# Head writes issued from GpSimd and three attentions run as one sequence, in a fused streaming-encoder layer

## The chip, the cores and the metric

The kernel runs on one core of a Trainium2 chip. The metric is device time in microseconds (us) of one launch. The engines are named as the profile names them: PE (TensorE matmul), PEld (its weight loads), DVE (VectorE), ACT (ScalarE), POOL (GpSimd) and SP (SyncE, which here only issues DMAs).

## The reference

One layer with shared weights is computed for a prompt of 2048 rows and for a sample group of 8 x 16 rows that has caches. All is float32, with a model width of 1024.

```python
h = rms_norm(x, g1) * (1 + sc1) + sh1
cols = h @ w_in                    # columns of four mixers A, B, C, D, 4 heads of 64 each
oa = gated_delta_rule(cols_A)      # conv, chunked triangular solve, recurrent state
ob = stick_breaking(q, k, v)       # sigmoid(z) * running product of sigmoid(-z), strictly causal
oc = softmax(q k / 8 + f_q - f_k) v            # causal, forget bias f
od = softmax(q k / 8 + bias[rel]) v            # own chunk of 64 and 8 before it
mixed = concat(oa, *[rms_norm(o_head, merge_g) for o in (ob, oc, od)])
x = x + ga1 * (mixed @ w_o)
h = rms_norm(x, g2) * (1 + sc2) + sh2
a, b = split(causal_conv3(h @ w_up))           # the samples continue from state_ffn_conv
x = x + ga2 * ((silu(a) * b) @ w_down)
```

The outputs are x of both groups and the new caches and states.

## The kernel before

**Parts and streams.** The prompt is cut into four parts of 512 rows; the 128 sample rows go with the first part of the projection and with the last part of the feed-forward. Two generators emit the program. The *dense* stream is the projection of all parts (`proj_stage`, then `feed_stage`): for each part the product with `w_o`, the second norm, 44 column blocks of `w_up` with the convolution (`up`), and the products with `w_down` (`down`). Each float32 product is three matmuls of split values (hi*hi, hi*lo, lo*hi); in the first feed-forward part the split weights are written to DRAM (`keptw_up`, `keptw_down`, `keptw_o`) and in later parts they are loaded from there in pieces of 512 KB. The *mixers* stream (`mixers`) is for each part the delta rule and the attentions B, C, D of the prompt (`attn_prompt`), and in parts 1 to 3 the attention of the samples (`attn_samples`).

**Order of the work.** `weave` takes a step of the mixers, adds its pace (table `PACE`) to a debt and then takes dense steps until the debt is paid. A scheduler in the build then sets the order of the instructions on each engine; mixers have high priority. While part 3's mixers run, `Order.step` ties each dense step to the mixers step 12 before it (`LAG`). A part's feed-forward needs all of that part's `mixed` rows.

**An attention of a part.** Each call of `attn_prompt` opens a tile pool of its own and runs *units*: a head times two blocks of 128 queries (for B also times a segment of 512 keys). `front` of a unit computes scores (PE, tile `z`), and for B (`Stick.segment`) two sigmoids `sn` and `w` on ACT (L733, L734), a running product `pr` on DVE (L741) that starts from the earlier segment's `pr`, and a product on POOL (L743); for C and D (`Soft`) a sum with the bias tile `add` and a maximum on DVE (L773), then exponentials on ACT. `back` of the unit before runs beside it: transposes of the weights (`ptr`), split copies `wh` and `wl`, matmuls with V (`oT`), and for a head's last unit `head_norm`. At a head's end `start_k` loads the next head's `qT`, `kT` and `add`; `start_v` loads `vhl`. At the end of an attention the last `back` runs alone, the pool is closed, and the next attention opens its own.

**`head_norm`** (L863 to L875) loads the gain `hg` (one buffer), squares the head's rows into `nsq` (one buffer, POOL, L869), sums, takes a reciprocal root in 12 small POOL instructions (L214 to L217), scales (L873, L874), and writes `nsq` to `mixed` in DRAM with a DMA of 128 KB issued by SP (L875). SP issues everything in one order, so what stands behind an instruction that waits, waits as well.

**Tiles of the attentions.** `sn` has 2 buffers, `pr` 3, the bias of C one tile of up to 2048 columns, that of D two tiles of 640, `kT` and `vhl` have (segments + 1) buffers, but 4 for C in part 3; `w` has 6 (B), 12 and 11 (C in parts 2 and 3) and 8 (D).

**Others that the change touches.** `samples_steps` loads 512 cached keys at a time into `ck` (512 KB, one buffer) and transposes them in two PSUM tiles, one for each half of the columns. `up` in part 3 loads 16 rows of `state_ffn_conv` into `stn` (two buffers) and transposes them on PE (`ptr<-ident,stn`).

Of the kernel before, what the change touches and what calls it, by code (L numbers as in the profile page):

```python
# [15 lines left out]
P = 128  # L16
# [702 lines left out]
class Stick:  # L719
# [5 lines left out]
    def segment(self, c0, c1):  # L725
# [137 lines left out]
def head_norm(K, A, gi, h, oh, nt, dst):  # L863
# [11 lines left out]
    nc.sync.dma_start(out=dst, in_=sq)  # L875


def attn_prompt(K, g, part):


    nc = K.nc
    gi = "BCD".index(g)
    lo = (lambda i: max(0, i - 4)) if g == "D" else (lambda i: 0)
    mask = {"B": K.m_strict, "C": K.m_incl, "D": None}[g]
    j0, s0, s1 = 2 * part, lo(4 * part) // 4, part + 1
    A = Ctx()
    A.ev, A.pb, A.sb, A.vb = Eng(nc, 0.5), 3, 2, 2 + int(part > 1)
# [11 lines left out]
    def head(h):  # L899
# [4 lines left out]
        H.oh = A.sp.tile([P, 4, 64], F32, name="oh", bufs=2)  # L904
        if g == "C":
            fb = A.sp.tile([P, s1 * 512], F32, name="add", bufs=1)
            nc.sync.dma_start(out=fb.rearrange("p (t c) -> p t c", c=P),
                              in_=K.nF[0:16 * s1].rearrange("(t h) p -> h t p", h=4)[h:h + 1].to_broadcast([P, 4 * s1, P]))
            H.add = lambda a, b, c1: fb[:, a:b]
# [50 lines left out]
    def back(u):  # L960
# [6 lines left out]
        if u.last:  # L967
            u.st.V.finish(None if g == "B" else [w.rl for w in u.st.wts], H.oh, 4 * part)
            if jj == j0 + 1:
                yield  # L970
                r, c = 4 * part * P, (1 + gi) * 256 + H.h * 64
                head_norm(K, A, gi, H.h, H.oh, 4, K.mixed[r:r + 512, c:c + 64].rearrange("(t p) d -> p t d", p=P))

    units = []
    for h in range(4):
        hs = Ctx()
        hs.h = h
        for jj in (j0, j0 + 1):
            st = Ctx()
            for s in range(jj // 2, -1, -1) if g == "B" else [None]:  # L980
# [10 lines left out]
                u.end = u.last and jj == j0 + 1  # L991
                units.append(u)

    def start_k(u):
        H = u.hs.H = head(u.hs.h)
        for s in order:
            H.kT[s] = A.sp.tile([P, 512], F32R, name="kT", bufs=A.ring)
            nc.sync.dma_start(out=f(H.kT[s]).unsqueeze(1), in_=rows(K.kT[g][s], H.h))
        yield

    def start_v(u):
        H = u.hs.H
        for s in order:
            H.v[s] = A.sp.tile([P, 4, 2, 64], F32R, name="vhl", bufs=A.ring)
            nc.sync.dma_start(out=f(H.v[s]).rearrange("p t c d -> p (t c d)"), in_=K.vhl[g][H.h, s])
        yield

    with K.tc.tile_pool(name=f"a{g}{part}", bufs=2, side="right", reuse_waits="tile") as A.sp:
        yield from start_k(units[0])
        for n, u in enumerate(units):  # L1010
            u.H = u.hs.H
            parts = [(front(u), u.nf)]
            if n:
                b = units[n - 1]
                parts.append((back(b), len(b.groups) + b.last))
            yield from merge(*parts)
            if u.start:
                yield from start_v(u)
            if u.end and n + 1 < len(units):
                yield from start_k(units[n + 1])  # L1020
        yield from back(units[-1])
# [457 lines left out]
def attn_samples(K, g, beside):  # L1479

    A = Ctx()
    A.ev, A.wb, A.pb, A.sb = Eng(K.nc, 0.5), 2, 2, 1
# [6 lines left out]
def samples_steps(K, A, g):  # L1489
# [10 lines left out]
    for n, src in (("k", K.qs[g]), ("v", K.ks[g])):  # L1500
        t = sp.tile([P, 4 if n == "k" else 2, 256], F32, name="c" + n, bufs=1 if n == "k" else 2)[:, 0]
# [28 lines left out]
    def load(b, s):  # L1530

        t = sp.tile([P, 4, 256], F32, name="ck", bufs=1)
        nc.sync.dma_start(out=t, in_=ck[0, b, s * 512:(s + 1) * 512].rearrange("(t p) h d -> p t (h d)", p=P))
        return t
# [7 lines left out]
    def keys(L, b, s):  # L1542

        L.kT[s] = []
        for u in range(2):
            k = load(b + u, s)
            kT = sp.tile([P, 2, 512], F32, name="ckT", bufs=2)
            L.kT[s].append(kT)
            for x in range(2):
                pt = psum()  # L1550
                for j in range(4):
                    K.pe.transpose(pt[:, j * P:(j + 1) * P], k[:, j, x * P:x * P + P], K.ident)
                A.ev.copy(kT[:, x], pt)
                yield
# [216 lines left out]
def feed_block(K, B, sa, sp, nxt, pool, copies):  # L1771
# [112 lines left out]

    def up(fi):
# [6 lines left out]
        if smp:  # L1892
            us = u[:, 2 + Tp:2 + Tp + NB * 18].rearrange("p (b s) -> p b s", s=18)
            parts.append((lambda i: us[:, :, i:i + 16], s16(yv[:, Tp:T])))
            stn = sp.tile([16, P], F32, name="stn", bufs=2)
            nc.sync.dma_start(out=stn, in_=I["state_ffn_conv"][0, :, :, fi * P:(fi + 1) * P].rearrange("b r c -> (b r) c"))
# [132 lines left out]
def mixers(K, G, p):  # L2029
# [20 lines left out]
    if p == 0:  # L2050
        yield from B
# [4 lines left out]
        yield from rest()  # L2056
    elif p == 1:
        yield from beside(B, 79, 1)
        yield from rest()
        yield from samples()  # L2060
    else:
        yield from samples()
        yield from B
        yield from rest()
# [97 lines left out]
```

## Time and profile before

| what | value |
|---|---|
| median of 3 runs | 3899.07 us (3897.04 to 3899.76) |
| the profiled execution | 3892.44 us, its span 3890.7 us |
| PE busy | 3628.3 us, 93% of the span |
| DVE, ACT, POOL busy | 2437.3, 1537.0, 1406.7 us |
| mean granted TensorE clock | 0.967 |

Busy time is the union of an engine's instructions; what PE lacks to the span is idle time, and only that can be gained without removing matmuls. A granted clock of 0.5 means that matmuls then run at half rate, so a stall costs its own length and some more. A row of waits tells which instruction waited and what came last before it could start. "DMA kT<-kTD" is a transfer into tile `kT`; its row in the timeline is the issue, not the landing. The stretches in the table of windows are: projection with parts 0 and 1 of the mixers (0 to 1150), samples B and C beside the first feed-forward part (to 1870), part 2's attentions (to 2430), samples D, delta rule and attention B of part 3 (to 2960), C (to 3200), D and the step to the last feed-forward part (to 3330), and that part (to the end).

### The profile page before, as it was taken

Reading aid. Unit: us, or ns where it says so; the run is one execution under the profiler, and the core shown is the slowest. Engines: PE = TensorE matmul, PEld = TensorE weight load, DVE = VectorE, ACT = ScalarE, POOL = GpSimd, SP = SyncE. Lnnn points to the kernel's source line nnn. Section 1 sums busy time; section 2 is a strip of 40 time slices with the busy share of each in tenths; the row PEclk is TensorE's granted clock in tenths of the full one; section 3 lists DMA queues with packets and bytes.
Section 4 is the critical chain, followed back from the end, with each engine's and each line's share of the span. In section 5 each row is a group of like instructions: output and inputs, shape, how many; then the busy total and the mean of one; then the engine's idle time right before and its main releaser. Section 6 shows DMA issues by size and latency. Waiting matters only on the chain.

```text
span 3890.7 us, 66224 instructions
## 1 busy us (share of the span) xinstructions
PE 3628.3 (93%) x22763; PEld 3147.3 (81%) x22763; DVE 2437.3 (63%) x5592; ACT 1537.0 (40%) x3352; POOL 1406.7 (36%) x3487
## 2 busy tenths in 40 slices
PE   6998899989988999999999999989999987899999
PEld 4887889989986667767877888668887876899999
DVE  5668556465676876877595656755875665344344
ACT  3455223343454533543463533413553443232221
POOL 4456244363333444434571112323652122122121
PEclk7999999999998999999999999999999998899999
DMA  7887868877668798987536555665445545444442
GB/s 225 290 279 245 300 199 299 295 256 246 218 227 255 254 307 274 306 293 270 200 120 213 171 201 169 226 209 178 158 148 182 177 123 206 141 149 137 153 143 93
DMA packets 529077, 830.36 MB, mean 213 GB/s; under 512 B 112651, under 2 KB 351260, under 8 KB 528477
## 3 DMA queue, kind: packets, MB, share of 16 engines
q1 hardware_dynamic: 527269, 825.16, 64.2%
q8 instruction: 181, 2.97, 0.3%
q0 software_dynamic: 1472, 0.97, 0.1%
q14 instruction: 155, 1.26, 0.1%
HBM read 611.81 MB, written 224.16 MB: 215 GB/s over the span
## 4 chain that ended last, share of the span: by engine, by line
PE 62%; DMA 11%; DVE 9%; POOL 4%; issue 3%; ACT 2%; SPq 1%; POOLq 0%; DVEq 0%; ACTq 0%
PE d L89 44%; PE z L89 5%; PE oT L89 5%; PE ptr L92 4%; PE ptr L89 2%; PE d L92 1%; DVE pr L741 1%; DMA w<-win 1%; DMA add<-nF 1%; DVE gy L1184 1%; DVE cv L1913 1%; DMA wraw<-in_ada_w_dram 1%; DMA raw<-in_x_prompt_dram 1%; PE z L92 1%; DVE acc L1823 1%
## 5 line engine op out<-in xcount | busy, mean ns | idle before, releaser
L89 PE MATMUL d<-hh,wu 128*128 128x512 f32 (+1 forms) x3520 | 1013.9, 364 | 2.8 <-DMA wu<-keptw_up 1.6
L89 PEld LDWEIGHTS d<-hh,wu 128*128 128x128 f32 x3520 | 635.2, 190 | 94.6 <-issue 8.6
L89 PE MATMUL d<-w,hh 128*128 128x256 f32 (+2 forms) x3536 | 679.3, 288 | 30.3 <-DMA w<-win 9.7
L89 PE MATMUL d<-hl,wu 128*128 128x512 f32 (+1 forms) x1760 | 638.8, 363 | 0.8 <-DVE hl L1863 0.7
L89 PEld LDWEIGHTS d<-w,hh 128*128 128x128 f32 x3536 | 557.6, 191 | 48.6 <-DVE w L459 11.8
L89 PE MATMUL d<-gh,wd 128*128 128x512 f32 (+1 forms) x1760 | 529.8, 369 | 10.3 <-DVE acc L1823 8.1
L89 PE MATMUL d<-w,hl 128*128 128x256 f32 (+2 forms) x1768 | 502.3, 286 | 0.2 <-DVE hl L408 0.2
L1913 DVE SCALAR_TENSOR_TENSOR cv<-u,fcw,cv 128x512 f32<-128x512 f32 (+1 forms) x440 | 300.1, 705 | 174.2 <-ACT cv L1911 170.9
L1823 DVE SCALAR_TENSOR_TENSOR acc<-d,mod,acc 128x512 f32<-128x512 f32 (+2 forms) x432 | 280.8, 656 | 188.4 <-PE d L89 187.1
L89 PEld LDWEIGHTS d<-hl,wu 128*128 128x128 f32 x1760 | 334.0, 190 | 43.9 <-DVE hl L1863 3.0
L89 PEld LDWEIGHTS d<-gh,wd 128*128 128x128 f32 x1760 | 319.1, 189 | 60.3 <-DVE acc L1823 13.6
L89 PEld LDWEIGHTS d<-w,hl 128*128 128x128 f32 x1768 | 336.3, 191 | 4.8 <-issue 3.3
L89 PE MATMUL d<-gl,wd 128*128 128x512 f32 (+1 forms) x880 | 319.4, 363 | 0.0
L89 PE MATMUL z<-kT,qT 128*128 128x512 f32 (+3 forms) x864 | 255.8, 385 | 34.7 <-DMA kT<-kTD 13.8
L840 ACT CAST wh<-ptr 128x512 fp32r<-128x512 f32 (+1 forms) x372 | 197.4, 552 | 226.8 <-PE ptr L92 133.6
L841 DVE TENSOR_TENSOR wl<-ptr,wh 128x512 fp32r<-128x512 f32 (+1 forms) x372 | 232.3, 639 | 79.5 <-ACT wh L840 69.1
L1900 ACT COPY u<-d 128x512 f32<-128x512 f32 (+1 forms) x220 | 109.9, 500 | 396.5 <-PE d L89 391.0
L92 PE MATMUL ptr<-ident,w 128*128 128x128 f32 x1448 | 225.1, 277 | 18.9 <-POOL w L743 8.2
L741 DVE TENSOR_TENSOR_SCAN pr<-sn,pr,zeros 128x512 f32<-128x512 f32 (+3 forms) x172 | 217.8, 1275 | 24.3 <-ACT sn L733 18.8
L1915 POOL COPY hal<-u 128x2 f32<-128x2 f32 x176 | 44.5, 254 | 519.7 <-ACT u L1900 516.2
L743 POOL TENSOR_TENSOR w<-w,pr 128x512 f32<-128x512 f32 (+3 forms) x168 | 190.8, 1138 | 112.1 <-DVE pr L741 60.2
L790 ACT ACTIVATE w<-w,nm 128x512 f32<-128x512 f32 (+3 forms) x284 | 174.1, 615 | 120.5 <-DVE nm L783 98.1
(610 smaller groups left out, 7116.5 us busy)
## 6 DMA issues: line engine op xcount, KB each, us to landing
wu<-keptw_up SPq DMA_DIRECT2D x264, 512.0 KB
w<-win SPq DMA_DIRECT2D x132, 512.0 KB
wd<-keptw_down SPq DMA_DIRECT2D x132, 512.0 KB
keptw_up<-wu SPq DMA_DIRECT2D x88, 512.0 KB
wu<-keptw_o SPq DMA_DIRECT2D x48, 512.0 KB
win<-w SPq DMA_DIRECT2D x44, 512.0 KB
raw<-in_w_up_dram SPq DMA_DIRECT2D x88, 256.0 KB
keptw_down<-wd SPq DMA_DIRECT2D x44, 512.0 KB
```

The costliest lines, as they stand in the source:

```text
L89: return self.note(self.nc.tensor.matmul(out, lhsT, rhs, **k))
L92: return self.note(self.nc.tensor.transpose(*a, **k))
L741: nc.vector.tensor_tensor_scan(out=pr[:, 0:m][:, ::-1], data0=sn[:, :m][:, ::-1], data1=K.zeros[:r, :m], initial=carry, op0=ALU.mult, op1= ...
L743: nc.gpsimd.tensor_tensor(w[:, :m], w[:, :m], pr[:, 1:m + 1], op=ALU.mult)
L790: self.K.nc.scalar.activation(w, w, AF.Exp, bias=self.nm, accum_out=self.l[:, s:s + 1])
L840: nc.scalar.copy(wh[:, c0:c1], pt[:, c0:c1])
L841: nc.vector.tensor_tensor(wl[:, c0:c1], pt[:, c0:c1], f(wh[:, c0:c1]), op=ALU.subtract)
L1184: nc.vector.scalar_tensor_tensor(yc, tap(c, i), self.cw[:, c, i:i + 1], yc, op0=ALU.mult, op1=ALU.add)
L1823: nc.vector.scalar_tensor_tensor(acc[k][:, c0:m], ps[:, :m - c0], gate[:, k, 0:1], acc[k][:, c0:m], op0=ALU.mult, op1=ALU.add)
L1900: nc.scalar.copy(u[:, 2 + c0:2 + m], ps[:, :m - c0])
L1913: nc.vector.scalar_tensor_tensor(o, tap(i), cw[:, i:i + 1], o, op0=ALU.mult, op1=ALU.add)
L1915: nc.gpsimd.tensor_copy(K.hal[:, fi], tail)
```

## The change

1. **Head writes.** `head_norm` issues the write to `mixed` from POOL. The gain `hg` (now 2 buffers) is loaded with the head's `qT`.
2. **One sequence.** In parts 2 and 3 B, C and D are one call of `attn_prompt(K, "BCD", p)`: one pool, one list of units, so that `start_k` of C's first head is emitted at the end of B's last unit, and B's last `back` runs beside C's first `front`; likewise C and D. `kT` and `vhl` have 4 buffers, `w` 10. `sn`, `pr`, C's bias and D's bias share one ring `aux` of 5 tiles of 640 columns. Parts 0 and 1 keep three calls and their buffers.
3. **C's bias** is loaded in pieces of 512 columns (one per segment) instead of in one DMA.
4. **Cached keys** of the samples come in two tiles of 256 keys (`ck`, two buffers); each is transposed into one PSUM tile.
5. **`stn`** is loaded three blocks ahead (four buffers).

The core of the diff:

```diff
@@ Stick.segment
-        sn = A.sp.tile([P, 512], F32, name="sn", bufs=A.sb)[:r]
+        sn = A.aux("sn", 512)[:r]
         w = A.w(m)[:r]
-        pr = A.sp.tile([P, 520], F32, name="pr", bufs=A.pb)[:r]
+        pr = A.aux("pr", 520)[:r]
@@ head_norm
-    mg = A.sp.tile([P, 64], F32, name="hg", bufs=1)
-    nc.sync.dma_start(out=mg, in_=K.I["merge_g"][0, gi, h:h + 1].to_broadcast([P, 64]))
...
-    nc.sync.dma_start(out=dst, in_=sq)
+    nc.gpsimd.dma_start(out=dst, in_=sq)
@@ attn_prompt
+def attn_prompt(K, gs, part):
+    A = Ctx()
+    A.ev, A.vb = Eng(K.nc, 0.5), 2 + int(part > 1)
+    A.psum = lambda: K.mps("z")
+    A.w = lambda m: A.sp.tile([P, 512], F32, name="w", bufs=A.wb)
+    if len(gs) > 1:
+        A.ring, A.wb = 4, 10
+        A.aux = lambda name, n: A.sp.tile([P, 640], F32, tag="aux", name=name, bufs=5)[:, :n]
+    else:
...
+    with K.tc.tile_pool(name=f"a{gs}{part}", bufs=2, side="right", reuse_waits="tile") as A.sp:
+        units = [u for g in gs for u in attn_units(K, A, g, part)]
+        a, b = units[0], units[-1]
+        yield from lab(K.nc, f"{a.g}{part}", a.start_k(a))
+        for n, u in enumerate(units):
+            yield from lab(K.nc, f"{u.g}{part}", attn_unit(units, n))
+        yield from lab(K.nc, f"{b.g}{part}", b.back(b))
+
+def attn_unit(units, n):
+    u = units[n]
+    u.H = u.hs.H
+    parts = [(u.front(u), u.nf)]
+    if n:
+        b = units[n - 1]
+        parts.append((b.back(b), len(b.groups) + b.last))
+    yield from merge(*parts)
+    if u.start:
+        yield from u.start_v(u)
+    if u.end and n + 1 < len(units):
+        yield from units[n + 1].start_k(units[n + 1])
@@ head, in attn_units
+        H.mg = A.sp.tile([P, 64], F32, name="hg", bufs=2)
+        nc.sync.dma_start(out=H.mg, in_=K.I["merge_g"][0, gi, h:h + 1].to_broadcast([P, 64]))
         if g == "C":
-            fb = A.sp.tile([P, s1 * 512], F32, name="add", bufs=1)
...
+            fb = [A.aux("add", 512) for _ in range(s1)]
+            for s in range(s1):
+                nc.sync.dma_start(out=fb[s].rearrange("p (t c) -> p t c", c=P),
...
-            bias = A.sp.tile([P, 640], F32, name="add", bufs=2)
+            bias = A.aux("bias", 640)
@@ samples_steps: load
-        t = sp.tile([P, 4, 256], F32, name="ck", bufs=1)
...
+        ts = [sp.tile([P, 2, 256], F32, name="ck", bufs=2) for _ in range(2)]
+        for n, t in enumerate(ts):
+            c = s * 512 + n * 256
...
@@ feed_block
+    for _ in range(3):
+        state_load()
...
-            stn = sp.tile([16, P], F32, name="stn", bufs=2)
...
+            stn = state.pop(0)
+            state_load()
@@ mixers
     else:
         yield from samples()
-        yield from B
-        yield from rest()
+        yield from attn_prompt(K, "BCD", p)
```

How this moves instructions is shown at three places, all in part 3. First the queue of SP where attention D follows C (`qTD`, `kTD`, `skew` are D's; `wu` and `wd` are weights of the dense stream). Before:

```order
L1801 DMA wu<-keptw_up 128x1024 x6
L875 DMA mixed<-nsq 128x4x64
L903 DMA qT<-qTD 128x1024
L912 DMA add<-skew 128x640
L998 DMA kT<-kTD 128x512 x2
L1005 DMA vhl<-vhlD 128x512 x2
```

and now:

```order
L1015 DMA kT<-kTC 128x512
L937 DMA qT<-qTD 128x1024
L1830 DMA wu<-keptw_up 128x1024
L940 DMA hg<-in_merge_g_dram 128x64
L949 DMA bias<-skew 128x640
L1830 DMA wu<-keptw_up 128x1024 x2
L1978 DMA wd<-keptw_down 128x1024 x2
L1022 DMA vhl<-vhlC 128x512 x2
L1978 DMA wd<-keptw_down 128x1024 x2
L1015 DMA kT<-kTD 128x512
```

Before, D's first loads stood behind the write of C's last head; now that write is not in this queue, and D's loads stand among the last loads of C.

Second, PE at the end of part 3's attentions (`oT<-...,os` is the last attention matmul, `raw` are the rows of `mixed` and of x for the last feed-forward part, `mh` and `ml` its first product). Before:

```order
L89 MATMUL oT<-wl,vhl 128x256
L89 MATMUL oT<-j_676,os 128x64 x2
L92 MATMUL ptr<-ident,stn 128x16 x4
L92 MATMUL d<-ident,raw 128x128 x80
L89 MATMUL d<-mh,wu 128x320
```

and now (the rows left out are `d<-gh,wd` and `d<-gl,wd`, with those shown 39 matmuls in all):

```order
L89 MATMUL oT<-j_676,os 128x64 x2
L89 MATMUL d<-gh,wd 128x512 x3
...
L89 MATMUL d<-gh,wd 128x512
L92 MATMUL d<-ident,acc 128x128 x16
L89 MATMUL d<-gh,wd 128x512
...
L89 MATMUL d<-gh,wd 128x512
L92 MATMUL d<-ident,acc 128x128 x16
L92 MATMUL d<-ident,raw 128x128 x80
L89 MATMUL d<-mh,wu 128x320
```

What is left of the third feed-forward part now stands behind the last attention matmul, and the transposes of `stn` are gone from this place.

Third, the queue of SP at the same place (`keptw_o` are the weights of the first product). Before:

```order
L1735 DMA out_dram<-raw 128x512 x4
L1801 DMA wu<-keptw_o 128x1024 x8
L1896 DMA stn<-in_state_ffn_conv_dram 16x128 x2
L867 DMA hg<-in_merge_g_dram 128x64
L875 DMA mixed<-nsq 128x4x64
L1937 DMA wd<-keptw_down 128x1024 x6
L1896 DMA stn<-in_state_ffn_conv_dram 16x128 x2
L875 DMA mixed<-nsq 128x4x64
L1896 DMA stn<-in_state_ffn_conv_dram 16x128
L1690 DMA raw<-mixed 128x512 x8
```

and now:

```order
L1764 DMA out_dram<-raw 128x512 x4
L1719 DMA raw<-mixed 128x512 x7
L1764 DMA out_dram<-raw 128x512 x3
L1719 DMA raw<-mixed 128x512 x3
L1764 DMA out_dram<-raw 128x512
L1719 DMA raw<-in_x_prompt_dram 128x512 x4
L1719 DMA raw<-in_x_sample_dram 128x512
L1719 DMA raw<-in_x_prompt_dram 128x512
L1830 DMA wu<-keptw_o 128x1024
L1719 DMA raw<-in_x_prompt_dram 128x512
L1830 DMA wu<-keptw_o 128x1024
L1719 DMA raw<-in_x_prompt_dram 128x512 x2
```

The weights of the first product, which stood ahead of the last two head writes, now stand behind the rows of `mixed`.

More of the change, by code (lines that the diff above doesn't have):

```diff
@@ L971, in back, with start_k, start_v @@
                 r, c = 4 * part * P, (1 + gi) * 256 + H.h * 64
-                head_norm(K, A, gi, H.h, H.oh, 4, K.mixed[r:r + 512, c:c + 64].rearrange("(t p) d -> p t d", p=P))
+                head_norm(K, A, H.mg, H.oh, 4, K.mixed[r:r + 512, c:c + 64].rearrange("(t p) d -> p t d", p=P))
+    def start_k(u):
+        H = u.hs.H = head(u.hs.h)
+        for s in order:
+            H.kT[s] = A.sp.tile([P, 512], F32R, name="kT", bufs=A.ring)
+            nc.sync.dma_start(out=f(H.kT[s]).unsqueeze(1), in_=rows(K.kT[g][s], H.h))
+        yield
+    def start_v(u):
+        H = u.hs.H
+        for s in order:
+            H.v[s] = A.sp.tile([P, 4, 2, 64], F32R, name="vhl", bufs=A.ring)
+            nc.sync.dma_start(out=f(H.v[s]).rearrange("p t c d -> p (t c d)"), in_=K.vhl[g][H.h, s])
+        yield
     units = []
@@ L991, in attn_prompt @@
                 u.end = u.last and jj == j0 + 1
+                u.g, u.front, u.back, u.start_k, u.start_v = g, front, back, start_k, start_v
                 units.append(u)
[L994 to L1021, printed above, removed]
+    return units
 def gate_tiles(K, cp):
@@ L1481, in attn_samples @@
     A = Ctx()
-    A.ev, A.wb, A.pb, A.sb = Eng(K.nc, 0.5), 2, 2, 1
+    A.ev, A.wb = Eng(K.nc, 0.5), 2
+    A.aux = lambda name, n: A.sp.tile([P, n], F32, name=name, bufs={"sn": 1, "pr": 2}[name])
     A.psum = lambda: K.mps("ptr")
@@ L1500, in samples_steps @@
     for n, src in (("k", K.qs[g]), ("v", K.ks[g])):
-        t = sp.tile([P, 4 if n == "k" else 2, 256], F32, name="c" + n, bufs=1 if n == "k" else 2)[:, 0]
+        t = sp.tile([P, 2, 256], F32, name="c" + n, bufs=2)[:, 0]
         nc.sync.dma_start(out=t, in_=src)
@@ L1545, in keys @@
         for u in range(2):
[L1546 removed]
             kT = sp.tile([P, 2, 512], F32, name="ckT", bufs=2)
             L.kT[s].append(kT)
[L1549 removed]
+            for n, k in enumerate(load(b + u, s)):
                 pt = psum()
[L1551 to L1553 removed]
+                for x in range(2):
+                    for j in range(2):
+                        c = (2 * x + j) * P
+                        K.pe.transpose(pt[:, c:c + P], k[:, j, x * P:x * P + P], K.ident)
+                A.ev.copy(kT[:, :, n * 256:n * 256 + 256], pt.rearrange("p (x n) -> p x n", x=2))
                 yield
@@ L1883, in carry, with state_load @@
         late.clear()
+    state, ahead_of = [], [c for j in range(NF) for c in (j, NF + j)] if smp else []
+    def state_load():
+        if ahead_of:
+            fi = ahead_of.pop(0)
+            state.append(sp.tile([16, P], F32, name="stn", bufs=4))
+            nc.sync.dma_start(out=state[-1], in_=I["state_ffn_conv"][0, :, :, fi * P:(fi + 1) * P].rearrange("b r c -> (b r) c"))
+    for _ in range(3):
+        state_load()
     def up(fi):
@@ L2055, in mixers @@
         yield from rule
-        yield from rest()
+        yield from chain(*[attn_prompt(K, g, p) for g in "CD"])
     elif p == 1:
-        yield from beside(B, 79, 1)
-        yield from rest()
+        yield from beside(attn_prompt(K, "B", p), 79, 1)
+        yield from chain(*[attn_prompt(K, g, p) for g in "CD"])
         yield from samples()
```

33 lines of the change are left out of this document (13 added, 20 removed).

## The prediction

> **What bounds the kernel now.** I read the page first, then the table of windows by stage, then the waits of PE in the stages that lack most, then the timeline there.
>
> ```profile
> span 3890.7 us, 66224 instructions
> PE 3628.3 (93%) x22763; PEld 3147.3 (81%) x22763; DVE 2437.3 (63%) x5592; ACT 1537.0 (40%) x3352; POOL 1406.7 (36%) x3487
> ```
> ```profile
> core 0: us, PE busy (x) PEld busy (x) DVE busy (x) ACT busy (x) POOL busy (x), PEclk, DMA share, GB/s
> 0.00:1150.00 1150.00, 1046.57 (x8101) 979.10 (x8101) 711.67 (x1805) 472.63 (x1056) 512.29 (x1462) 0.96 0.77 258
> 1150.00:1870.00 720.00, 670.46 (x3603) 503.11 (x3604) 520.17 (x1077) 314.17 (x625) 299.51 (x569) 0.96 0.83 276
> 1870.00:2430.00 560.00, 544.31 (x2896) 457.41 (x2894) 372.75 (x809) 245.06 (x534) 193.13 (x467) 0.98 0.54 178
> 2960.00:3200.00 240.00, 226.55 (x1223) 191.25 (x1222) 145.61 (x372) 107.06 (x242) 34.13 (x114) 0.97 0.56 170
> 3200.00:3330.00 130.00, 90.55 (x539) 77.70 (x539) 73.27 (x258) 47.94 (x133) 28.17 (x115) 0.83 0.56 195
> 3330.00:3891.00 561.00, 550.60 (x3685) 535.35 (x3683) 242.95 (x591) 132.32 (x310) 115.76 (x296) 0.99 0.41 132
> ```
>
> PE is the bound: it lacks 262 us of the span (3890.7 - 3628.3), and the change removes no matmul. So its gain is idle time of PE, and the half clock that follows it. Most of the 262 lies where the change does little: 103 us before 1150. In the stages whose attentions it rebuilds, part 2 lacks only 16 us of 560; attention C of part 3 lacks 13 of 240; attention D with the step to the last feed-forward part lacks 39 of 130, at a granted clock of 0.83. The last part lacks 10 of 561, so earlier `stn` loads can gain nothing once it runs. The waits of PE from 2960 to 3330 name the stalls:
>
> ```profile
> PE ptr L92 <- DMA stn<-in_state_ffn_conv_dram: 18.3, 2, 9.6
> PE z L89 <- DMA kT<-kTD: 13.8, 1, 13.8
> PE z L89 <- DVE mx L773: 5.8, 5, 2.3
> PE z L89 <- DMA kT<-kTC: 5.3, 1, 5.3
> ```
>
> The first of these stands for something else. Transposes of `stn` were queued on PE where the attentions end, but without them PE would have waited there all the same, as the timeline of the last heads shows:
>
> ```profile
> 3283.64 3.96 SPq L1801 DMA_DIRECT2D wu<-keptw_o  x8
> 3287.12 0.66 PE L89 MATMUL oT<-j,os 128*128 128x64 f32 x4 [0.52 <-DVE os L71]
> 3287.82 0.47 DVE L860 TENSOR_SCALAR oh<-oT,rl 128x64 f32<-128x64 f32 x2 [0.75 <-PE oT L89]
> 3291.83 0.39 SPq L875 DMA_DIRECT2D mixed<-nsq  x1
> 3298.88 0.61 POOL L869 TENSOR_TENSOR nsq<-oh 128x256 f32<-128x256 f32 x1 [8.78 <-DMA mixed<-nsq]
> ...
> 3304.45 0.72 POOL L874 TENSOR_TENSOR nsq<-nsq,hg 128x256 f32<-128x256 f32 x1 [0.54 <-DMA wd<-keptw_down]
> 3305.20 0.39 SPq L875 DMA_DIRECT2D mixed<-nsq  x1
> 3307.26 4.22 SPq L1690 DMA_DIRECT2D raw<-mixed  x8
> 3310.01 2.03 PE L92 MATMUL d<-ident,raw 128*128 128x128 f32 x8 [2.98 <-DMA raw<-mixed]
> 3327.49 0.41 PE L89 MATMUL d<-mh,wu 128*128 128x320 f32 x1
> ```
>
> The write of the third head, issued behind 4 MB of weights, took 7.05 us to free `nsq` (3291.83 to 3298.88); only then could the last head be normed, written and read back. PE, with nothing else queued, had its last attention matmul at 3287.12 and its first product of the next part at 3327.49, 40.4 us later.
>
> **The change part by part.** *The end of part 3 (one sequence, order on PE and SP).* Now 39 matmuls of 512 columns and 32 transposes stand behind the last attention matmul. Their rates:
>
> ```profile
> 2702.24 19.13 PE d L89 x84
> ```
> ```profile
> 3278.23 0.82 PE L92 MATMUL d<-ident,acc 128*128 128x128 f32 x6
> ```
>
> 39 x 19.13/84 = 8.9 us and 32 x 0.82/6 = 4.4 us, together 13.3 us of work that was elsewhere and now fills the hole. The chain from the last attention matmul stays: to the end of L860 1.2 us (3288.29 - 3287.12), from L869 to the end of L874 6.3 us (3305.17 - 3298.88), the issue and landing of the write, and from the first read of `mixed` to the first product 20.2 us (3327.49 - 3307.26). SP's last write took 2.06 us from issue to that read. For a DMA issued by POOL the nearest rows are these small loads, and the slowest one:
>
> ```profile
> L293 POOL DMA_DIRECT2D abia<-in_ada_b_dram x16: 520/587/611, 72.8 to 494.0; - x16
> ...
> DMA to landing us min/median/max: 2.7/5.1/6.3
> ```
> ```profile
> smask<-in_smask_dram POOLq DMA_DIRECT2D x1, 90.0 KB, 11.0
> ```
>
> The issue costs 0.6 us. For the landing I take 8 us, between 5.1 (9 KB) and 11.0 (90 KB), nearer to the latter in size (bounds 2.7 and 11.0). The Trainium skill ("DMA: Bandwidth & Descriptors", section "Anatomy of one DMA — SWDGE (gpsimd) path") fits such a DMA as 2.0 us plus bytes / 436e3, which as an estimate for 128 KB is 2.3 us. By it the sum would gain 5.7 us more, but the trace's 5.1 us for only 9 KB does not agree. The weights `keptw_o` now come behind the rows: two pieces behind 16 pieces of 256 KB are 5.2 MB, at the 308 GB/s of this row 17 us, so hidden by the 20.2; for all eight pieces, 8.4 MB, 27 us.
>
> ```profile
> 3292.00:3320.00 28.00, 9.65 (x45) 8.10 (x45) 7.24 (x15) 5.23 (x10) 3.70 (x14) 0.51 0.87 308
> ```
>
> I add 2 us (0 to 7). So 1.2 + 6.3 + 0.6 + 8 + 20.2 + 2 = 38.3 us, and the gain is 40.4 + 13.3 - 38.3 = 15.4 us (7 to 23).
>
> *D's start.* D's loads stood on SP behind the write of C's last head:
>
> ```profile
> 3208.84 0.37 SPq L875 DMA_DIRECT2D mixed<-nsq  x1
> 3210.34 0.86 SPq L998 DMA_DIRECT2D kT<-kTD  x2
> 3215.05 1.83 PE L89 MATMUL z<-kT,qT 128*128 128x512 f32 x4 [13.76 <-DMA kT<-kTD]
> ```
> ```profile
> 3203.00:3221.00 18.00, 5.95 (x16) 4.88 (x17) 3.28 (x10) 0.00 (x0) 4.44 (x22) 0.53 0.62 217
> ```
>
> They now stand among C's last loads, with weights of the dense stream between them. The wait of 13.8 goes, and of the 5.95 us of matmuls at clock 0.53 about 2.5 are lost to the clock: 16.3 us. What is late next is the back of C's last unit, which has dense matmuls beside it; if these are used up earlier, some 4 us return (12 to 16).
>
> *C's start.* 5.3 us and about 2 of clock, 7 us (4 to 8). *C's heads.* The bias came as one tile of 1 MB that had to be free as a whole; now the first piece has the ring's fifth tile, the others follow segment by segment. Of the 5.8 us behind L773 and some 2 of clock I take half, 4 us (0 to 8).
>
> *Part 2.* Its starts are covered by dense work already; these waits from 1870 to 2500 bear on it, and I take 2 us (0 to 5):
>
> ```profile
> PE d L89 <- DMA wu<-keptw_up: 1.6, 1, 1.6
> ...
> PE z L89 <- DMA kT<-kTC: 1.1, 1, 1.1
> ```
>
> *Cached keys.* From 1150 to 1870 PE waited for them and their copies 10.2 us:
>
> ```profile
> PE ptr L92 <- DMA ck<-in_cache_sb_k_dram: 7.1, 2, 3.6
> ...
> PE ptr L92 <- DVE ckT L71: 3.1, 2, 2.3
> ```
>
> Two half tiles let one land while the other is transposed; DMA is 0.83 busy there, so I take half, 5 us (0 to 11).
>
> *What it costs.* POOL issues 48 writes of 0.6 us, 28 us on an engine that is 36% busy, and SP loses as many; none lies ahead of a waiting POOL instruction, since the write follows L874 in its own queue. I take 1 us (0 to 5). The shared ring costs B: tiles are taken in the order sn, pr, sn, pr, so `sn` of a segment takes the tile of the `pr` three segments back, which the scan of the segment just before still reads as its start. So ACT can't run ahead of DVE, which it did:
>
> ```profile
> 2812.46 0.60 ACT L733 ACTIVATE sn<-z 128x512 f32<-128x512 f32 x1 [3.48 <-PE z L89]
> 2813.69 1.36 DVE L741 TENSOR_TENSOR_SCAN pr<-sn,pr,zeros 128x512 f32<-128x512 f32 x1
> 2816.07 0.65 ACT L733 ACTIVATE sn<-z 128x512 f32<-128x512 f32 x1
> ```
>
> The 112 segments of parts 2 and 3 (48 and 64) then need 0.60 + 1.36 us in turn, some 2 us, and in these rows they are 3.6 us apart (2812.46 to 2816.07). PE's dense matmuls cover the rest; I take 4 us (0 to 67, the rival below).
>
> The sum: 15.4 + 16.3 + 7 + 4 + 2 + 5 - 1 - 4 = 45 us. The profiled execution, 3892.44 us with its span of 3890.7, would be 3847; it lies 6.6 below the median of the runs, 3899.07, and from that the time is 3854 us.
>
> **The rivals.** *The shared ring stops B (slower).* Every `sn` waits for the scan before it, behind the dense stream's ACT and DVE work, PE meets the late weights in its fixed order, and no dense matmul stands in between: 112 x 0.60 = 67 us. With the other terms (49) that is 3899 - 49 + 67 = 3917 us. It decides from 57 us of such waits on, when the kernel is slower by 0.2%. For it: DVE is the busiest engine after PE, and the rows above show ACT ahead by 2.6 us (this `sn` began at 2812.46; with the ring it would wait for the scan that ends at 2815.05). Against: segments 3.6 us apart leave 1.6 us of slack in each. Chance 0.07.
>
> *The stalls come back inside C and D.* Loads, bias pieces and weights now share SP's queue closely, and a piece that waits for its tile holds the weights behind it; the gains other than D's start cancel against new waits of 1 to 3 us at heads: 45 - 27 = 18 us, 3881 us. For it: the order shows a weight between almost any two loads of an attention. Against: the windows show DMA 0.56 busy. Chance 0.20.
>
> *Software writes land late.* `nsq` has one buffer, so the next L869 holds POOL until the write has landed, and the last chain holds PE. At twice the slowest row, 22 us, the end of part 3 loses 14: 3868 us. The Trainium skill (same page, section "SWDGE vs HWDGE vs iDMA") says that POOL's descriptors are written to rings in SBUF, from which a busy DVE can lock it out, and so speaks against this edit; no row here shows 128 KB written that way. Chance 0.09.
>
> *New waits eat all of it,* within 0.2%: 0.07. That the change doesn't do what it says is out: the order shows it.
>
> **How the numbers follow.** About 0.2%, 7.8 us, is what a measurement of this kernel can tell from no change. The forecast, 3854 (3838 to 3872), has 0.57. Faster: 0.57 + 0.20 + 0.09 = 0.86; same 0.07; slower 0.07. The range 3838 to 3884 takes in the forecast's bounds, the late writes and most of the second rival.
>
> **What would show it.** Right: no wait of PE over 3 us from B's start in part 3 to the last `raw` but the one for `mixed`; that one under 10; the stretch from the last attention matmul to the first `mh` product 34 to 42 us; D's and C's starts without a half clock; PE's idle down by some 35 to 45. Wrong: idle in B of part 3 above 20 us with waits on `sn` or `pr`; landings of POOL's writes above 15 us; an end that is later by waits for `keptw_o`.

## The result and the profile after

The changed kernel takes 3855.74 us (median of 4 runs, 3853.66 to 3866.20) against 3898.30 us (4 runs, 3897.04 to 3899.76): a ratio of 0.9895, interval 0.988 to 0.9911. That is 42.6 us less. The forecast was 3854 us, 45 us less. Its profiled execution took 3866.20 us, the longest of its four runs, as that of before was shorter than its other runs; so the two traces differ by 26.3 us of span only, and each stretch has to be looked at by itself. The page after, its span and the busy times:

```profile
span 3864.4 us, 66383 instructions
...
PE 3651.4 (94%) x22763; PEld 3165.5 (82%) x22763; DVE 2451.7 (63%) x5592; ACT 1534.6 (40%) x3350; POOL 1458.6 (38%) x3535
```

PE has the same 22763 matmuls and lacks 213.0 us of the span (3864.4 - 3651.4), where it lacked 262. But its busy time is 23.1 us longer (3651.4 - 3628.3) with the same work, so the granted clock is the first thing to look at. The windows by stage (columns as before: busy time of each engine, granted clock, DMA share, GB/s):

```profile
0.00:1150.00 1150.00, 1050.30 (x8012) 983.94 (x8013) 705.25 (x1772) 462.20 (x1038) 520.90 (x1464) 0.94 0.76 255
1150.00:1870.00 720.00, 679.73 (x3560) 504.97 (x3559) 522.94 (x1087) 316.09 (x625) 297.04 (x578) 0.95 0.82 272
1870.00:2430.00 560.00, 538.27 (x2946) 452.32 (x2945) 391.04 (x877) 254.13 (x568) 213.23 (x504) 0.98 0.56 184
2960.00:3200.00 240.00, 240.00 (x1337) 206.56 (x1337) 161.62 (x438) 115.16 (x270) 45.24 (x140) 1.00 0.57 186
3200.00:3330.00 130.00, 119.60 (x689) 103.99 (x688) 64.77 (x169) 42.66 (x101) 32.93 (x102) 0.96 0.56 195
```

Two things have moved. From 2960 to 3200 PE is busy in all 240 us at full clock (it lacked 13 at 0.97), and from 3200 to 3330 it lacks 10 (it lacked 39 at 0.83): the stalls that the prediction priced are gone. Up to 1150 us the clock went the other way, 0.96 to 0.94, and fewer matmuls are done by then (8012 against 8101). The waits of PE from 2980 to 3310, where `kT<-kTD`, `kT<-kTC` and the maximum of L773 headed the list:

```profile
PE d L92 <- DMA raw<-in_x_prompt_dram: 3.2, 3, 1.5
PE d L92 <- DVE raw L71: 2.0, 1, 2.0
PE d L89 <- ACT gh L2015: 1.8, 1, 1.8
```

Nothing there lasts over 2.0 us at a time, and the wait for `mixed` is not in the list. The timeline shows D's start of part 3, now without a wait, and the end of the attentions (issues of SP and POOL are `DMA_DIRECT2D` rows; a bracket gives the idle time before a row and what ended it):

```profile
3121.15 0.42 SPq L1015 DMA_DIRECT2D kT<-kTD  x1
3128.36 0.62 PE L89 MATMUL z<-kT,qT 128*128 128x512 f32 x2
...
3261.85 0.65 PE L89 MATMUL oT<-j,os 128*128 128x64 f32 x4
3262.54 0.48 DVE L860 TENSOR_SCALAR oh<-oT,rl 128x64 f32<-128x64 f32 x2 [0.75 <-PE oT L89]
3269.61 0.73 POOL L873 TENSOR_TENSOR nsq<-nsq,hg 128x256 f32<-128x256 f32 x1 [0.61 <-DVE nsq L872]
3270.63 0.79 POOL L874 DMA_DIRECT2D mixed<-nsq  x1 [0.29 <-POOL nsq L873]
3274.04 3.35 SPq L1719 DMA_DIRECT2D raw<-mixed  x7
3278.89 1.04 PE L92 MATMUL d<-ident,raw 128*128 128x128 f32 x8
3288.61 0.42 SPq L1830 DMA_DIRECT2D wu<-keptw_o  x1
3290.10 1.14 SPq L1719 DMA_DIRECT2D raw<-in_x_prompt_dram  x2
3297.53 1.94 PE L92 MATMUL d<-ident,raw 128*128 128x128 f32 x8 [1.47 <-DMA raw<-in_x_prompt_dram]
3300.14 1.09 PE L92 MATMUL d<-ident,raw 128*128 128x128 f32 x4 [0.67 <-DVE acc L71]
3300.88 0.61 PE L89 MATMUL d<-mh,wu 128*128 128x320 f32 x1
```

From the last attention matmul to the first product of the last part it still takes 39.0 us (3300.88 - 3261.85; 40.4 before), but PE works through most of it, as one row of windows for this stretch in each kernel shows. Before:

```profile
3287.50:3327.50 40.00, 16.23 (x88) 12.41 (x87) 13.62 (x37) 9.83 (x28) 5.41 (x20) 0.66 0.85 304
```

and after:

```profile
3262.20:3300.90 38.70, 28.30 (x155) 21.46 (x154) 22.54 (x49) 13.11 (x33) 5.81 (x18) 0.91 0.73 257
```

PE has 155 instructions in it where it had 88: the 39 matmuls and 32 transposes of the prediction came in, 4 transposes of `stn` left.

Now the whole span by stretches. "Idle" is the sum of PE's gaps between its matmuls, "half clock" is half of PE's busy time in stretches of granted clock 0.5, about what that clock cost (a little less in truth: in the trace of before, matmuls `d<-w,hh` of 256 columns start 119 ns apart at a granted clock of 1.0 and 213 ns apart at 0.5). Both are summed from the records of the two traces:

| stretch | idle before, after | half clock before, after | forecast gain |
|---|---|---|---|
| to the first product of the second feed-forward part | 143.1, 138.4 | 54.0, 81.9 | 4 |
| part 2, B's first score to D's last | 13.9, 11.6 | 4.2, 6.7 | 2 |
| from there to B of part 3 | 25.0, 23.2 | 10.3, 8.4 | - |
| B of part 3 | 5.8, 6.9 | 2.9, 4.3 | -4 |
| to C's first score | 5.3, 0 | 0, 0 | 7 |
| C | 8.2, 0.6 | 5.8, 0 | 4 |
| to D's first score, and D | 14.3, 0 | 2.6, 0 | 16.3 |
| D's last score to the first product of the last part | 25.2, 10.4 | 4.5, 2.8 | 15.4 |
| the last part | 5.1, 4.6 | 3.6, 5.1 | - |

Between the first products of the second and of the last feed-forward part the kernel went from 1446.3 to 1392.6 us, 53.7 us less. Ahead of that it came 27.1 us later (1881.2 to 1908.3). The question for the experiments is therefore double: which edits made the 54 us, and what was lost before.

### The profile page after: what moved, and what is told of

It reads as the page before. It is cut to its first block, busy times and chain, and to the rows that moved or that the text cites. A ratio compares the mean times of both kernels' runs of the same rounds, so it can differ in the third digit from the quotient of the medians.

```text
span 3864.4 us, 66383 instructions
## 1 busy us (share of the span) xinstructions
PE 3651.4 (94%) x22763; PEld 3165.5 (82%) x22763; DVE 2451.7 (63%) x5592; ACT 1534.6 (40%) x3350; POOL 1458.6 (38%) x3535
## 4 chain that ended last, share of the span: by engine, by line
PE 60%; DVE 7%; DMA 4%; POOL 3%; issue 2%; ACT 1%; SPq 0%; DVEq 0%; POOLq 0%; ACTq 0%
PE d L89 43%; PE z L89 5%; PE oT L89 5%; PE ptr L92 4%; DVE pr L741 2%; PE ptr L89 2%; PE d L92 1%; DMA raw<-in_x_prompt_dram 1%; DVE cv L1954 1%; PE z L92 1%; DVE wl L841 1%; DMA out_dram<-raw 1%; POOL w L743 1%; DVE acc L1852 0%; DMA sadd<-nFs 0%
## 5 line engine op out<-in xcount | busy, mean ns | idle before, releaser
L89 PE MATMUL d<-w,hh 128*128 128x256 f32 (+2 forms) x3536 | 695.3, 292 | 31.1 <-DMA w<-win 9.2
L89 PEld LDWEIGHTS d<-w,hh 128*128 128x128 f32 x3536 | 572.1, 196 | 46.9 <-DMA w<-win 10.4
L89 PE MATMUL d<-w,hl 128*128 128x256 f32 (+2 forms) x1768 | 510.7, 290 | 0.2 <-DVE hl L408 0.2
L89 PEld LDWEIGHTS d<-w,hl 128*128 128x128 f32 x1768 | 344.5, 195 | 7.1 <-issue 5.6
L741 DVE TENSOR_TENSOR_SCAN pr<-sn,pr,zeros 128x512 f32<-128x512 f32 (+3 forms) x172 | 227.0, 1327 | 39.2 <-ACT sn L733 26.6
L1956 POOL COPY hal<-u 128x2 f32<-128x2 f32 x176 | 47.6, 270 | 512.8 <-ACT u L1941 512.2
```

Of the source, the lines that this page charges most:

```text
L89: return self.note(self.nc.tensor.matmul(out, lhsT, rhs, **k))
L741: nc.vector.tensor_tensor_scan(out=pr[:, 0:m][:, ::-1], data0=sn[:, :m][:, ::-1], data1=K.zeros[:r, :m], initial=carry, op0=ALU.mult, op1= ...
L1956: nc.gpsimd.tensor_copy(K.hal[:, fi], tail)
```

## The experiments

Ratios are to the kernel before on the same chip. The marks are from each profiled execution: the first product of the second feed-forward part, and the time from it to the first product of the last one.

| kernel | ratio (95% interval) | mark | from mark to last part |
|---|---|---|---|
| before, again | 1.0010 (0.9996 to 1.0023) | 1890.8 | 1449.9 |
| changed, again | 0.9876 (0.9861 to 0.9891) | 1906.9 | 1389.2 |
| changed, third chip | 0.9898 (0.9882 to 0.9915) | 1908.0 | 1392.3 |
| the sequence alone | 0.9853 (0.984 to 0.9866) | 1887.6 | 1395.1 |
| all but the sequence | 0.9948 (0.9935 to 0.996) | 1896.1 | 1421.6 |
| the shared ring alone | 1.0012 (1.0002 to 1.0022) | 1886.0 | 1460.1 |
| changed, SP writes | 0.9857 (0.9835 to 0.9879) | 1877.5 | 1397.2 |
| changed, whole key tiles | 0.9858 (0.9836 to 0.9881) | 1884.2 | 1389.6 |
| the sequence and early `stn` | 0.9858 (0.9837 to 0.9878) | 1882.3 | 1397.9 |
| changed, late `stn` | 0.9895 (0.9878 to 0.9911) | 1893.6 | 1393.1 |
| B apart, C and D joined | 0.9913 (0.9897 to 0.993) | 1884.3 | 1417.1 |
| B and C joined, D apart | 0.9959 (0.9945 to 0.9973) | 1890.0 | 1432.0 |

**The changed kernel again**, unedited.

> The changed kernel once more, for a second profile. Between the first product of the second feed-forward part and that of the fourth, the first profile took 53.7 us less than before (idle time of PE down by 44.7), but up to the second part's first product it was 27 us later than before, on 2 us more of idle before 630 and 24 us more at half clock in the first 630 us. Theory A (that delay is mostly chance of the clock in the one profiled execution, which at 3866.2 us was the slowest of its four): 3850 to 3858 us, the second part's first product at 1881 to 1895 us. Theory B (the early edits cost it): the same 1900 to 1912 us again. Both: 50 to 57 us less between the two products.

Measured: 3859.23 us against 3904.12. The late mark repeats within 1.4 us (1906.9), as theory B has it, and the gain behind it is there again: 57.1 us against the first profile of before.

**The sequence alone**: the changed kernel with SP's head writes, whole key tiles and two `stn` again. It keeps the early load of `hg` and the bias of C in pieces.

```diff
-    nc.gpsimd.dma_start(out=dst, in_=sq)
+    nc.sync.dma_start(out=dst, in_=sq)
@@ samples_steps: load
-        ts = [sp.tile([P, 2, 256], F32, name="ck", bufs=2) for _ in range(2)]
+        t = sp.tile([P, 4, 256], F32, name="ck", bufs=1)
@@ up
-            stn = state.pop(0)
-            state_load()
+            stn = sp.tile([16, P], F32, name="stn", bufs=2)
```

> The changed kernel with SP's head writes, whole tiles of cached keys and two stn tiles as before, so that the one sequence and C's bias in pieces are left of the change. My theory (the gain is idle time of PE in parts 2 and 3 that the one sequence removes; the other edits give nothing): 3845 to 3862 us. Rival (the writes issued by POOL, which free SP's queue, carry a good part): 3870 us or more.

Measured: 3849.81 us (3847.36 to 3851.16) where the changed kernel, on the same chip, took 3857.05 to 3861.45. So the sequence, with C's bias in pieces, is enough for all of the gain, and the other edits together took 9 us of it back. This kernel beats both.

**All but the sequence**: three calls with the old buffers, and the other edits.

```diff
-        yield from attn_prompt(K, "BCD", p)
+        yield from chain(*[attn_prompt(K, g, p) for g in "BCD"])
```

> The changed kernel with three separate attentions in parts 2 and 3 and their buffers of before, so that head writes from POOL, C's bias in pieces, halves of cached keys and early stn loads are left. My theory: 3885 to 3905 us, with the waits for kT of D (13.8 us) and for the last head write back again. Rival (these edits carry a good part): 3860 to 3880 us.

Measured: 3886.31 us, a gain of 20 us (0.0052 of 3899). That is inside my range, but one of the two waits that I expected did not come back. The waits of PE in D of part 3 show where one part of it went:

```profile
PE z L89 <- DVE mx L773: 5.8, 1, 5.8
...
PE z L89 <- DMA kT<-kTD: 0.5, 1, 0.5
```

With the write on POOL, SP is free for D's loads, and the wait of 13.8 us for `kTD` is gone without any sequence; a wait of 5.8 for a maximum inside D takes part of its place. Inside C, with the bias in pieces and no sequence, idle fell from 8.2 to 1.8 us and the half clock from 5.8 to 2.1. The hole at the end stayed: 21.6 us idle of 37.8.

**The shared ring alone**, in the kernel before:

```diff
-        sn = A.sp.tile([P, 512], F32, name="sn", bufs=A.sb)[:r]
+        sn = A.sp.tile([P, 640], F32, tag="aux", name="sn", bufs=5)[:r] if A.shared else A.sp.tile([P, 512], F32, name="sn", bufs=A.sb)[:r]
@@ the same for pr
+    A.shared = g == "B" and part > 1
```

> The kernel before, in which sn and pr of attention B in parts 2 and 3 alone share one ring of five tiles. My estimate of this cost: 4 us, 3896 to 3908 us. Rival (each of 112 segments waits 0.6 us on the path): 3940 us or more; were the ring a gain, the kernel before would be faster by over 8 us.

Measured: 1.0012, 5 us (1 to 9). The forecast's 4 us lies within this. The rival with 67 us falls. Where the 5 us go is not shown: in this kernel's profile B of part 3 lost no more than before (5.6 us of idle and 3.1 of half clock, 5.8 and 2.9 before).

**One early edit undone at a time.** First the head writes on SP again:

```diff
-    nc.gpsimd.dma_start(out=dst, in_=sq)
+    nc.sync.dma_start(out=dst, in_=sq)
```

> The changed kernel, but with the head writes issued by SP again. Theory M: of the early edits the head writes on POOL cost most of the some 10 us by which the changed kernel is later than the one with the sequence alone, through half clock before attention C of part 0. Then C's first score matmul of part 0 stands at 632 to 638 us (644.5 in the changed kernel, 634.0 with the sequence alone), and the time is 3851 us (3846 to 3855). Rival N: POOL's writes cost nothing there and the half tiles of cached keys do: that mark stays at 641 or later and the time is 3856 to 3862.

Then the cached keys in one tile again, with the rest of the change:

```diff
-        ts = [sp.tile([P, 2, 256], F32, name="ck", bufs=2) for _ in range(2)]
+        t = sp.tile([P, 4, 256], F32, name="ck", bufs=1)
```

> The changed kernel, but with the cached keys in one tile of 512 again. The forecast had them gain 5 us. Theory M: they cost some 4 us instead: the stretch between the first products of the first and the second feed-forward part falls from 729-731 us to 723-726, and the time to 3855 us (3851 to 3859), with the wait of PE for the transfer into ck back at 6 to 9 us. Rival: they gain what was forecast, and without them the time is 3862 to 3866.

Then the sequence with only the early `stn` beside it (SP writes and whole key tiles):

> The one sequence together with the early loads of stn, with SP's head writes and whole tiles of cached keys. Theory M: the early loads bring nothing, since the wait named after stn stood for the chain of the last head: 3850 us, within 4 of the kernel with the sequence alone (3849.8), and the stretch from the last attention matmul to the first product of the last part stays at 44 to 47 us. Rival: the wait was for stn itself: that stretch falls to 36 to 41 us and the time to 3840 to 3845.

And the changed kernel with `stn` as before:

```diff
-            stn = state.pop(0)
-            state_load()
+            stn = sp.tile([16, P], F32, name="stn", bufs=2)
```

> The changed kernel, but with stn loaded as before (two buffers). What the early edits cost was gone both without POOL's head writes and without the half tiles of cached keys. Theory M: these two cost it together, by the order that they give parts 0 and 1, and stn has no share: ratio 0.987 to 0.990, as the changed kernel. Rival: it takes all three, so that any edit that reorders the program lands on another phase of the clock: ratio 0.985 to 0.9865.

Measured: 3842.14, 3841.25 and 3843.34 us on one chip (0.9857, 0.9858, 0.9858), and 3855.71 (0.9895) for the last. The first three are shorter than my theories had them (the third has the time of its rival, but not the short stretch at the end that the rival asks for); a part of this is the chip, on which before took 3898.14 us and not 3904.12 as on that of the first four kernels. None of the forms "this edit costs so much" fits. Without POOL's writes the loss is gone; without the half tiles, with POOL's writes kept, it is gone too; `stn` has no share, and its early loads bring nothing (3843 beside 3842 and 3841; the stretch at the end 44.0 us, 45.2 with the sequence alone). POOL's writes and the half tiles cost time only together.

**Both kernels on other chips.** The changed kernel on the chip of the last four kernels:

> The changed kernel on a chip that also runs the next three. Four kernels that lack one or more of its early edits stand at ratios of 0.9853 to 0.9858, the changed kernel at 0.9895 and 0.9876. Theory M: it is later by some 8 to 12 us in the first two parts, whatever the chip: ratio 0.987 to 0.990, C's first score matmul of part 0 at 641 to 647 us. Rival: that was chance of two chips: ratio 0.985 to 0.9865 and the mark at 630 to 638.

Measured: 3859.72 us, 0.9898, its mark at 1908.0. The loss of the pair is then between 0.0018 (0.9876 - 0.9858) and 0.0045 (0.9898 - 0.9853), 7 to 18 us. And the kernel before:

> The kernel before itself, as a second look at how far the marks of one program move. Theory M: the phase of the clock gate moves them by several us: C's first score matmul of part 0 at 627 to 637 us, and the first product of the second feed-forward part at 1881 to 1890. Rival: both are fixed within 2 us by the program (626.7 and 1881.2), so that all that the other kernels show there is cost of their edits. Time against the kernel before: ratio 1.000, within 0.001.

Measured: 1.001, no difference; but its first score of C in part 0 came at 637.2 us (626.7 in the first profile), and its mark 9.6 us later. One program moves by 10 us before that mark. The windows from 0 to 630 us, in which granted clock and matmuls done go roughly together: before, twice,

```profile
0.00:630.00 630.00, 545.24 (x4074) 496.31 (x4074) 399.21 (x879) 251.61 (x524) 299.23 (x734) 0.94 0.79 261
```
```profile
0.00:630.00 630.00, 548.10 (x3986) 499.27 (x3987) 389.60 (x861) 248.53 (x517) 291.13 (x713) 0.91 0.78 255
```

the changed kernel, first profile and third chip,

```profile
0.00:630.00 630.00, 542.85 (x3934) 495.98 (x3934) 395.02 (x855) 243.13 (x513) 291.12 (x706) 0.90 0.77 252
```
```profile
0.00:630.00 630.00, 542.34 (x3931) 496.20 (x3931) 396.81 (x855) 243.05 (x513) 291.14 (x702) 0.91 0.77 252
```

and without POOL's writes:

```profile
0.00:630.00 630.00, 547.23 (x4044) 498.76 (x4045) 394.75 (x867) 249.99 (x520) 295.09 (x726) 0.93 0.79 259
```

PE is idle about as long in all of them up to the mark (135 to 143 us, 126 without POOL's writes), but the half clock cost 81.9, 76.1 and 78.2 us in the three profiles of the changed kernel, 54.0 and 68.3 in before, 58.6 without POOL's writes, 63.7 without the half tiles. The Trainium skill ("TensorE: Matmul & The Clock Gate", section "What's actually happening") says that the clock follows a free-running window of activity and that one kernel meets it in different phases from run to run; the two profiles of before agree with it. So a part of the late mark is clock. But it can't be all of the loss: the kernel with `stn` as before has both edits and the ratio of the changed kernel (0.9895), and it lost only 65.2 us to half clock up to its mark, less than the second profile of before. Whether the pair itself makes the clock worse is not shown.

**What the half tiles cost on PE.** Another part of the loss is work that takes PE longer at full clock. Between the first products of the first and of the second feed-forward part every kernel here runs the same 3627 matmuls. PE's busy time there, less the half clock, is 660.7 to 662.5 us in the six profiles of kernels with half tiles and 650.5 to 654.1 us in the eight without, so 7 to 12 us come with this edit and with no matmul more. (The sentence ahead of the change, that only idle time can be gained without removing matmuls, does not hold here.) More than half of it stands in one group, the scores of the samples with the cached keys. These are the rows of the groups from 1150 to 1910 us (count, then busy time and mean ns of one, then idle time before), before and after:

```profile
L89 PE MATMUL ptr<-ckT,qb 128*32 128x512 f32 x128 | 23.1, 633 | 2.4 <-ACT ckT L73 1.6 <-DVE ckT L71 0.8
```
```profile
L89 PE MATMUL ptr<-ckT,qb 128*32 128x512 f32 x128 | 29.0, 633 | 2.3 <-DVE ckT L71 2.3
```

One matmul takes as long as before, but fewer of them overlap. Each has weights of only 32 columns, and up to four run side by side. Call those that follow one another on PE with no other matmul between them a row: in a row of eight, four start 7 ns apart and the other four 453 ns after the first. So a row of two takes PE as long as a row of eight, as the timeline of the changed kernel shows:

```profile
1219.34 1.06 PE L89 MATMUL ptr<-ckT,qb 128*32 128x512 f32 x8
...
1324.08 1.04 PE L89 MATMUL ptr<-ckT,qb 128*32 128x512 f32 x2
```

The 128 matmuls stand on PE in 23 rows in every kernel with whole key tiles, in 29 in those with half tiles and in 31 in the one with half tiles and SP's writes; six rows more at about 1 us each are the 5.9 us between 23.1 and 29.0. That this edit costs no time without POOL's writes goes with PE's idle time in this stretch: it was 35.3 us in that kernel (one profile) and 42.0 to 47.6 us in all others. Why POOL's writes keep that gain away is not shown.

**The seams.** The kernel with the sequence alone, cut at one seam in parts 2 and 3. B by itself:

```diff
-        yield from attn_prompt(K, "BCD", p)
+        yield from chain(*[attn_prompt(K, g, p) for g in ('B', 'CD')])
```

> The kernel with the sequence alone (ratio 0.9853), but with B by itself, with its own sn and pr, and only C and D as one sequence. Theory M: in part 3 the wait for kT of C's start comes back (4 to 6 us, 5 to 8 with the half clock), B gets back the 2 to 4 us that the ring cost it; D's start and the end keep what they gained: ratio 0.986 to 0.987 (3 to 6 us later). Rival: a separate start of C also takes away the dense work that stood behind the last attention matmul, and 15 us more return at the end: ratio 0.9895 or more.

and D by itself, with ('BC', 'D') in the same line:

> The kernel with the sequence alone (ratio 0.9853), but with D by itself. Theory M: D's start of part 3 waits 11 to 15 us again for its kT behind the write of C's last head, 13 to 17 with the half clock, and the end keeps its gain: ratio 0.9885 to 0.990. Rival: what stands behind the last attention matmul now came from there, so that both return: 28 to 32 us, ratio 0.9925 or more. Third way: D's loads find another cover and nothing returns: ratio below 0.9865.

Measured: 3863.53 us (0.9913) and 3883.24 us (0.9959): cutting before C gives back 0.0060, 23 us, cutting before D 0.0106, 41 us. My theory was wrong in both, and the rival right. The waits of PE, B by itself (2920 to 3305):

```profile
PE ptr L92 <- DMA stn<-in_state_ffn_conv_dram: 22.4, 2, 14.8
...
PE z L89 <- DMA kT<-kTC: 1.6, 1, 1.6
```

D by itself (2600 to 3400):

```profile
PE ptr L92 <- DMA stn<-in_state_ffn_conv_dram: 17.6, 2, 10.0
PE z L89 <- DMA kT<-kTD: 14.5, 1, 14.5
```

The start that was cut costs what it did (14.5 for D) or less (1.6 for C). What both have in common is the other row: the hole at the end is back, under the name of `stn`. Its windows, B by itself, and D by itself:

```profile
3262.10:3301.40 39.30, 14.67 (x88) 11.01 (x86) 13.25 (x36) 9.95 (x28) 3.71 (x14) 0.70 0.93 335
```
```profile
3282.80:3322.00 39.20, 15.56 (x88) 11.37 (x87) 13.34 (x37) 9.65 (x27) 4.56 (x16) 0.70 0.84 304
```

and with the sequence alone:

```profile
3237.50:3282.70 45.20, 34.04 (x173) 26.17 (x172) 24.68 (x50) 14.32 (x35) 7.09 (x18) 0.84 0.64 224
```

With one seam open, no dense matmul is left behind the last attention matmul (88 instructions: 80 transposes of rows, 4 of `stn` and the last attention matmuls), as in the kernel before. With B, C and D as one, 57 dense matmuls and 32 transposes are left, because the attentions end earlier: 650.7 us after the first product of the third feed-forward part with the sequence alone, 692.5 and 697.1 with a seam, 710.2 before.

## Why the prediction was right, and where it was not

The total came out as forecast, 42.6 us for 45, by two errors that cancel: what the sequence gains was put too low (41 us, measured some 54), and what the early edits do had the wrong sign. That the total fits so closely is luck; that most of the gain comes from stalls of PE at the starts of C and D and at the end is not.

- **The end of part 3, 15.4 us.** Right in size: 14.8 us of idle and 1.7 of half clock, and by its mechanism, moved work. The two seams show that this term belongs to no single seam; any cut takes it away. Inside the chain one step was drawn wrong: the last write landed 4.6 us after its issue (at 3270.63), where I took 0.6 and 8, and nothing waited for it. Of the seven reads of `mixed` from 3274.04 the first five take the columns of A and B, which had been written long before, and the first that needs D's last head was issued behind them, at 3276.60. From the write's issue to the first product it was 30.2 us (3300.88 - 3270.63), where 0.6, 8, 20.2 and 2 make 30.8: that this agrees is luck. `keptw_o` cost nothing: the first product stands behind a transpose that waited for a copy of the x rows, which SP reads last.
- **D's start, 16.3 us.** Measured 13.8 of wait, and 3.1 of idle and half clock in D. Right. It has two sufficient causes, which the prediction did not say: the write off SP's queue (all but the sequence) or the loads ahead of it (the sequence with SP's writes).
- **C's start, 7 us.** Idle 5.3, and no half clock in work. Right, somewhat less.
- **C's heads, 4 us.** The step that took half of the wait and 2 us of clock was mis-sized: 7.6 of idle and 5.8 of half clock, 13.4 us. Most of it needs no sequence, since in the kernel without it 1.8 and 2.1 remained. That kernel has the bias in pieces, but also POOL's writes, and no run has one without the other there: with B by itself, which has the bias in pieces and SP's writes, 6.3 us of idle and 1.7 of half clock remained in C. Which of the two it is stays open.
- **Part 2, 2 us.** Idle 2.3 less, half clock 2.5 more: nothing.
- **The ring, -4 us.** Right in size: 5 us (1 to 9) by itself; in B of part 3 idle and half clock rose by 2.5.
- **Cached keys, 5 us, and POOL's writes, -1.** Wrong in sign. The wait for the transfer into `ck` fell from 7.1 to 3.0 us, as this row of the waits from 1150 to 1910 shows,

```profile
PE ptr L92 <- DMA ck<-in_cache_sb_k_dram: 3.0, 2, 2.4
```

  but the kernel without the half tiles is faster, not slower, by 7 us or more. The failed step is that the freed wait counted as time won and that the same matmuls were taken to cost PE the same. With half tiles the score matmuls stand in more and shorter rows, and PE was busy 7 to 12 us longer in that stretch. The prediction also took the clock of the first two parts as fixed; it cost 76 to 82 us in the changed kernel and 54 to 68 in the others, and how much of this is the edits' doing stays open.
- **The writes that land late** fell: the slowest of 48 took 8.0 us, the median 3.7 (below). The Trainium skill's fit ("DMA: Bandwidth & Descriptors", section "Anatomy of one DMA — SWDGE (gpsimd) path"), 2.3 us as an estimate for 128 KB, is too low, but nearer than my 8. Its section "SWDGE vs HWDGE vs iDMA" says that DVE locks POOL out of the memory of its rings during the 2-port perf mode, a condition that the prediction left out; no landing was longer than 8.0 us with DVE 63% busy, and no run here shows what the spread from 2.4 to 8.0 comes from.
- **The stalls that come back inside C and D** fell: PE idles 0.6 us in C and not at all in D.

The marks named for "right" were all met but one (the longest wait from B's start in part 3 to the last `raw` is 2.7 us): PE's idle fell by 49.9 us (245.7 to 195.8), more than 35 to 45, and the span did not follow, since the half clock took 23 us more.

## What to carry to other kernels

Where one engine is the bound and several chains run beside its filler work, joining the chains paid twice here: at the seams, and at the end, where the filler that was saved covers the last chain; with one seam cut the second part was gone, so such seams are not priced one by one. Read a stall's worth with the clock that it costs, and after an edit compare the granted clock of the stages that it was not meant for. An edit that only shortens a wait by 3 to 7 us can be lost in a change of clock of 10 us, or in the order that it gives the busy engine: here it split rows of small matmuls that run side by side. So compare the busy time at full clock of the same work too, try each such edit alone, and leave it out when it brings nothing.

## What the runs showed of the hardware that I had not expected

**Packets.** The head write has rows of 256 bytes. From the page of before and of after:

```profile
DMA packets 529077, 830.36 MB, mean 213 GB/s; under 512 B 112651, under 2 KB 351260, under 8 KB 528477
```
```profile
DMA packets 507063, 830.39 MB, mean 215 GB/s; under 512 B 89099, under 2 KB 327707, under 8 KB 506460
...
q0 software_dynamic: 3776, 7.27, 0.6%
```

The software queue had 1472 packets and 0.97 MB before: the 48 writes, issued by POOL, are 48 packets each of 2.7 KB (2304 packets, 6.30 MB). Against the changed kernel with SP's writes (113675 under 512 B) 24576 small packets are missing, 512 for each write: SP's form is a packet for each row. The write from POOL took 0.79 us to issue (SP's 0.37) and landed in 2.4, 3.7 and 8.0 us (least, median, most):

```profile
L874 POOL DMA_DIRECT2D mixed<-nsq x48: 788/793/849, 195.4 to 3270.6; - x48
...
DMA to landing us min/median/max: 2.4/3.7/8.0
```

**A clock of 0.95 that cost nothing.** In the profile of the sequence with early `stn`, 23 stretches, 2113 us in all, were recorded at a granted clock of 0.95; no other profile of this study has that level. The windows from 832 to 1139 us, of this kernel,

```profile
832.00:1139.00 307.00, 299.07 (x2377) 284.34 (x2376) 194.22 (x577) 144.71 (x349) 127.70 (x400) 0.95 0.71 233
```

and of the one with the sequence alone,

```profile
832.00:1139.00 307.00, 299.57 (x2380) 284.84 (x2379) 194.84 (x573) 144.72 (x352) 130.63 (x405) 1.00 0.71 234
```

and the groups of instructions in that window (count, then busy time and mean ns of one), of the same two kernels,

```profile
L89 PE MATMUL d<-w,hh 128*128 128x256 f32 x808 | 154.4, 285 | 1.1 <-DVE hl L408 0.9 <-DMA w<-win 0.2
```
```profile
L89 PE MATMUL d<-w,hh 128*128 128x256 f32 x808 | 154.2, 285 | 0.9 <-DVE hl L408 0.9
```

808 matmuls of one shape take 285 ns on average at both clocks. So a mean clock below 1 should be read by its stretches before it is called a cost.
